# Eight single PSUM banks around the seven-product FFN tiles, six ordinary tiles ahead of them, and adaLN weights in chunks of 1024 columns

## The chip, the cores and the metric

One Trainium2 (trn2) chip, of which the kernel uses 1 core. The metric is the device time in microseconds (us) of one execution, taken as the median of 3 runs. PE is the matmul engine (TensorE), DVE is VectorE, ACT is ScalarE, POOL is GpSimd, and SP is the engine whose queue issues most of the DMAs.

## The reference

The reference is one step of a two-layer recurrent decoder trunk, on a prompt of 512 tokens and on 8 samples of one token, 1024 features wide. Cut to what the change touches:

```python
mod = einsum('bd,de->be', silu(c), w_ada[l]) + b_ada[l]      # 6 chunks of 1024 per layer
sh_m, sc_m, gt_m, sh_f, sc_f, gt_f = split(mod, 6)
out = mixer(x * (1 + sc_m) + sh_m)                           # layer 0 even, layer 1 odd
x = layer_norm(ALPHA * x + (1 + gt_m) * out)
gate, up = split(einsum('bld,df->blf', x * (1 + sc_f) + sh_f, ffn_w_in[l]), 2)
x = layer_norm(ALPHA * x + (1 + gt_f) * einsum('blf,fd->bld', silu(gate) * up, ffn_w_out[l]))
```

`ffn_w_in[l]` is 1024 x 5632 (2816 gate and 2816 up columns, or 22 tiles of 128 of each), and all data are float32.

## The kernel before

Activations lie transposed, features on partitions, as tiles of 128 x 2 x 260: two halves of 256 prompt tokens and 4 samples. Each float32 product is made of three fast matmuls: a weight is split into a rounded part ("hi", a cast on ACT) and a remainder ("lo", a subtraction on DVE), an activation likewise, and PE adds hi*hi, hi*lo and lo*hi in PSUM (`mm3`, lines 284 to 288). The split costs ACT and DVE work for each weight, as well as PE three matmuls.

**Order of the work.** Weights come in the order of one list, `plan`, which is written out by hand. `WS.take` makes the split of the next unit with high priority and loads one entry ahead, into a ring of 3 raw buffers of 1 MB ("raw"); all its loads go through SP's queue (L208, L213). A scheduler at build time lays out one fixed order per engine from the priorities; at run time each engine goes through its order and waits for semaphores. A section under `high_priority(offset=3000)` goes ahead of ordinary work when both are ready.

**PSUM.** There are 8 banks of 2 KB per partition. `psum(2, 4, "g")` holds for the whole kernel: 2 tiles "acc" of two banks each (`acc_tile`) and 4 tiles "mx" of one bank (`mx`). A buffer is taken again once the tile before in it has been read for the last time.

**The adaLN rows** (`mod`) are made in the gaps of the plan. An "ada" entry is 128 rows x 2048 columns of `w_ada`; `ada_part` (L370) multiplies it in four column groups of the array at a time, 512 columns wide. After 8 entries `ada_rows` copies the sum out of PSUM, transposes it in 4 blocks into another mx tile and adds the bias. There are 40 entries: 16 in the even mixer, 16 in the first FFN, 8 in the input projection of the odd mixer.

**The seven-product tiles** are in the second layer's FFN alone. For tiles f = 0 to 3 (`SW0 = 4`) a tile is made the old way: one gate and one up unit of 8 x 6 matmuls, 96 in all. From f = 4 on, `sw_unit` (lines 929 to 967) treats gate and up columns, the two halves of the contraction and the two token halves as a 2 x 2 by 2 x 2 block product with seven multiplications (Strassen-Winograd form). Each is 12 matmuls (`prod`, lines 939 to 941), 84 in all. The activation sums `t1` to `t4` are made once (`t_forms`, 28 DVE operations). The weight sums are made for each tile by the generator `sw_weights`, in four steps: w1, then w2 with four sums in place in the raw buffer, then wu, then wg. The first step is made when the tile before is taken, and one more at each `ws.more()` inside that tile. w1 and w2 take their halves from a ring of 3 buffers ("whi", "wlo"); wu and wg from a ring of 4 ("wxh", "wxl").

In one tile the products run in this order: a (w1 lower), e (wu upper), b (wg lower, on top of a copy of a), a (w1 upper, on top), b (wu lower, on top), d (wg upper, on top of b + p5), c (w2 upper, on top of a copy of b). `o1` holds a and d, `o2` holds c and b, and e is an mx tile. At the end the gate `silu(o1)` is multiplied by the up values `o2`, and the product is split into ah and al for the second FFN matmul. The first half of the FFN (hb = 0) ends with tile 10, the second runs over tiles 11 to 21. In the first half ACT also does one `affine` of x per tile.

Of the kernel before, what the change touches and what calls it, by code (L numbers as in the profile page):

```python
# [35 lines left out]
SW0 = 4  # L36
# [4 lines left out]
def build(tc, I, O):  # L41
    nc = tc.nc
    V, S, G, T, SY = nc.vector, nc.scalar, nc.gpsimd, nc.tensor, nc.sync
    with ExitStack() as ctx:
# [86 lines left out]
        def bc(ap, shape):  # L131
            return ap.to_broadcast(shape)
# [49 lines left out]
        class WS:  # L182
# [77 lines left out]
            def ada(self):  # L260
                while self.i < len(units) and plan[units[self.i][0]][0] == "ada":
                    p_, _, r = self.take()
                    if p_[2] == 0:
                        self.acc = mx()
                    ada_part(self.acc, p_[2], r)
                    if p_[2] == 7:
                        ada_rows(self.acc, p_[6], p_[4] // 128)
# [27 lines left out]
        def p_ada(l, js):  # L295
            return [("ada", I["w_ada"][l], k, 1, D * j, 2 * D, l) for j in js for k in range(8)]
# [35 lines left out]
        plan += mix(p_cols("out", ev_out, (0, 256)), E4[4:6], 1) + E4[6:] + p_cols("out", ev_out, (512, 768))  # L332
# [35 lines left out]
        def ada_part(p, k, r):  # L368
            for c in range(4):
                T.matmul(p[32 * c:32 * c + 32, 0:512], condT[:, k, :], r[:, 0, 512 * c:512 * c + 512],  # L370
                         start=(k == 0), stop=(k == 7), tile_position=(0, 32 * c), skip_group_check=True)

        def ada_rows(p, l, j):
            sb = tmp.tile([128, 512], F32, tag="t2k", name="adarow")
            S.copy(sb, p)
# [3 lines left out]
            tt(mod[l][:, j:j + 16, :].rearrange("p (c b) r -> p b c r", b=4),  # L379
               q.rearrange("p (b c r) -> p b c r", b=4, r=32)[:, :, :, 0:9],  # L380
               bc(vA[:, 48 * l + j:48 * l + j + 16].rearrange("p (c b) -> p b c", b=4).unsqueeze(3), [128, 4, 4, 9]), ALU.add)
# [27 lines left out]
        ctx.enter_context(psum(2, 4, "g"))  # L409
# [472 lines left out]
        def ffn(l, mid=None):  # L882
            with tc.tile_pool(name=f"ff{l}", bufs=1, reuse_waits="tile") as fp:
# [47 lines left out]
                def sw_unit(f):  # L931
                    w1, w2, wu, wg = ws.get("sw", 128 * f)
                    t1, t2, t3, t4, b11, b21, b22 = tf
                    o1, o2, e = acc_tile(), acc_tile(), mx()[:, :HN]
                    a_, d_, c_, b_ = o1[:, 0, :HN], o1[:, 1, :HN], o2[:, 0, :HN], o2[:, 1, :HN]

                    def prod(out, w, off, t, st):
                        for k in range(4):
                            T.matmul(out, w[0][:, off + k], t[0][:, k], start=st and k == 0, stop=False, skip_group_check=True)  # L939
                            T.matmul(out, w[1][:, off + k], t[0][:, k], start=False, stop=False, skip_group_check=True)  # L940
                            T.matmul(out, w[0][:, off + k], t[1][:, k], start=False, stop=k == 3, skip_group_check=True)  # L941

                    soon = lambda: tc.high_priority(offset=HIGH)
                    prod(a_, w1, 0, b11, True)
                    with soon():
                        S.copy(b_, a_)
                    prod(e, wu, 4, t1, True)
                    p5 = t2k("p5")[:, 0]
                    with soon():
                        S.copy(p5, e)  # L950
# [12 lines left out]
                    with soon():  # L963
                        add(b_, b_, p5)
                    m = f % 11
                    fin_ev(0, m, 0, o1[:, :, :HN])
                    fin_ev(1, m, 0, o2[:, :, :HN])

                for hb in range(2):
# [12 lines left out]
                    def fin_ev(up, d, j, acc, hs=BOTH):  # L982
                        m = d + j
                        if up == 0:
# [3 lines left out]
                            if hb == 0 and 3 <= m <= 10:  # L988
                                affine(last["act"], [m - 3])
# [1138 lines left out]
        ffn(1)  # L2128

# [30 lines left out]
```

## Time and profile before

| what | value |
|---|---|
| runs | 1416.21 us median of 3 (1413.34 to 1416.77) |
| the profiled execution | 1415.38 us, of which the span is 1413.3 |
| PE, DVE, ACT, POOL busy | 94%, 62%, 39%, 14% of the span |
| granted TensorE clock, mean | 0.974 |
| DMA | 185 MB, q1 busy 37.4% of 16 engines' span |

A matmul's row shows its duration in the pipeline (0.28 us for 260 columns). Matmuls overlap, so the pace is read from starts, and idle time in a row of PE counts from the end of the duration, not from the time at which the next could have started. The number in brackets at the end of a timeline row is that idle time and what ended it.

### The profile page before, as it was taken

How to read it: one execution, taken by the hardware profiler on the slowest of the kernel's cores; microseconds unless marked ns; L12 is line 12 of the kernel's file. 1: busy time of each engine (PE TensorE's matmuls, PEld its weight loads, DVE VectorE, ACT ScalarE, POOL GpSimd, SP SyncE). 2: the span in 40 equal slices, each digit the busy share in tenths (PEclk: the TensorE clock that was granted, in tenths of full speed). 3: DMA queues.
4: the chain of work that ended last, by engine and by line, in shares of the span. 5: the costliest groups of instructions: out<-in, count | busy, mean ns of one | idle time of the engine just before them, and what ended most of it. 6: DMA issues, size and time to landing. Idle time of an engine off the chain costs nothing. (4 is left out here: it accounts for less than half of the span.)

```text
span 1413.3 us, 28868 instructions
## 1 busy us (share of the span) xinstructions
PE 1323.4 (94%) x12159; PEld 1237.9 (88%) x12159; DVE 875.0 (62%) x1947; ACT 555.9 (39%) x957; POOL 192.7 (14%) x215
## 2 busy tenths in 40 slices
PE   6898999989999999999998999999978899888996
PEld 4797986989998999999987989889978899888996
DVE  4667664687897233323682785677687634777465
ACT  3545535453333222222353223364445522555331
POOL 2200010350011200000250331114200000000013
PEclk9999999999999999999998999999979999999997
DMA  9653364313346742335449446532213133232311
GB/s 282 187 175 131 133 222 141 107 54 109 130 160 218 227 156 98 136 131 180 152 177 195 139 143 206 137 98 65 85 30 90 54 112 98 82 90 72 123 61 61
DMA packets 169147, 185.48 MB, mean 131 GB/s; under 512 B 18444, under 2 KB 153994, under 8 KB 163642
## 3 DMA queue, kind: packets, MB, share of 16 engines
q1 hardware_dynamic: 163034, 166.43, 37.4%
q0 software_dynamic: 5744, 17.08, 3.8%
q8 instruction: 95, 1.56, 0.4%
q14 instruction: 34, 0.28, 0.1%
q10 hardware_dynamic: 240, 0.13, 0.0%
HBM read 167.11 MB, written 15.36 MB: 129 GB/s over the span
## 5 line engine op out<-in xcount | busy, mean ns | idle before, releaser
L111 DVE TENSOR_TENSOR wlo<-raw,whi 128x1024 fp32r<-128x1024 f32 (+2 forms) x216 | 212.2, 993 | 179.5 <-ACT whi L242 133.6
L242 ACT CAST whi<-raw 128x1024 fp32r<-128x1024 f32 (+2 forms) x162 | 149.9, 933 | 419.6 <-PE acc L286 284.7
L284 PE MATMUL acc<-hhi,whi 128*128 128x260 f32 x1360 | 283.4, 289 | 2.7 <-ACT whi L242 1.3
L286 PE MATMUL acc<-hlo,whi 128*128 128x260 f32 x1360 | 282.6, 288 | 0.9 <-DVE hlo L111 0.9
L288 PE MATMUL acc<-hhi,wlo 128*128 128x260 f32 x1360 | 278.3, 285 | 0.0
L284 PEld LDWEIGHTS acc<-hhi,whi 128*128 128x128 f32 x1360 | 211.6, 190 | 22.9 <-issue 9.6
L286 PEld LDWEIGHTS acc<-hlo,whi 128*128 128x128 f32 x1360 | 212.4, 190 | 5.3 <-issue 2.1
L288 PEld LDWEIGHTS acc<-hhi,wlo 128*128 128x128 f32 x1360 | 211.8, 190 | 2.0 <-issue 1.3
L286 PE MATMUL acc<-al,whi 128*128 128x260 f32 x576 | 116.1, 283 | 3.3 <-DVE al L111 3.3
L284 PE MATMUL acc<-ah,whi 128*128 128x260 f32 x576 | 117.3, 285 | 1.0 <-DVE x L123 0.8
L288 PE MATMUL acc<-ah,wlo 128*128 128x260 f32 x576 | 114.9, 282 | 0.0
L284 PEld LDWEIGHTS acc<-ah,whi 128*128 128x128 f32 x576 | 88.7, 188 | 5.1 <-issue 2.6
L286 PEld LDWEIGHTS acc<-al,whi 128*128 128x128 f32 x576 | 88.7, 188 | 3.7 <-DVE al L111 3.5
L288 PEld LDWEIGHTS acc<-ah,wlo 128*128 128x128 f32 x576 | 88.3, 188 | 0.0
L111 DVE TENSOR_TENSOR smp<-acc,gt 128x8 f32<-128x8 f32 (+1 forms) x72 | 11.6, 161 | 117.6 <-PE acc L288 91.7
L863 PE MATMUL acc<-hhi,whi 128*128 128x260 f32 x208 | 59.9, 289 | 3.3 <-ACT hhi L821 3.3
L111 DVE TENSOR_TENSOR wxl<-raw,wxh 128x512 fp32r<-128x512 f32 (+1 forms) x82 | 62.1, 771 | 1.2 <-ACT wxh L242 1.0
L160 ACT CAST whi<-raw 128x512 fp32r<-128x512 f32 x54 | 31.7, 620 | 78.8 <-issue 50.7
L865 PE MATMUL acc<-hlo,whi 128*128 128x260 f32 x208 | 59.0, 291 | 3.2 <-DVE hlo L814 1.8
L111 DVE TENSOR_TENSOR sg<-acc,sg 128x520 f32<-128x520 f32 (+1 forms) x48 | 30.9, 651 | 45.7 <-PE acc L288 41.1
L864 PE MATMUL acc<-hhi,wlo 128*128 128x260 f32 x208 | 59.0, 286 | 0.0
L939 PE MATMUL acc<-hhi,whi 128*128 128x260 f32 x144 | 43.2, 300 | 10.1 <-DVE acc L111 10.1
(636 smaller groups left out, 2932.2 us busy)
## 6 DMA issues: line engine op xcount, KB each, us to landing
raw<-in_w_ada_dram SPq DMA_DIRECT2D x40, 1024.0 KB, 5.3
raw<-in_ffn_w_in_dram SPq DMA_DIRECT2D x24, 1024.0 KB, 5.0
raw<-in_ffn_w_in_dram SPq DMA_DIRECT2D x40, 512.0 KB, 3.9
raw<-in_ffn_w_out_dram SPq DMA_DIRECT2D x16, 1024.0 KB, 5.2
raw<-in_ev_w_in_dram SPq DMA_DIRECT2D x10, 1024.0 KB, 8.4
raw<-in_od_w_in_dram SPq DMA_DIRECT2D x10, 1024.0 KB, 5.7
raw<-in_w_ada_dram SPq DMA_DIRECT2D x16, 512.0 KB, 7.1
raw<-in_ffn_w_out_dram SPq DMA_DIRECT2D x16, 384.0 KB, 3.0
```

The lines of the kernel that those rows point to most:

```text
L111: V.tensor_tensor(out=out, in0=a, in1=b, op=op)
L160: S.copy(t[0][:, q], src[:, q])
L242: S.copy(hi[:, :nk, :m], rj)
L284: T.matmul(acc[:, hf, :HN], wh[:, k - koff, :], ah(k)[:, hf, :], start=st, stop=False)
L286: T.matmul(acc[:, hf, :HN], wh[:, k - koff, :], al(k)[:, hf, :], start=False, stop=False)
L288: T.matmul(acc[:, hf, :HN], wl[:, k - koff, :], ah(k)[:, hf, :], start=False, stop=sp)
L863: T.matmul(out, wh[:, k, :], ah(k)[:, hf, :], start=n == 0, stop=False)
L864: T.matmul(out, wl[:, k, :], ah(k)[:, hf, :], start=False, stop=False)
L865: T.matmul(out, wh[:, k, :], al(k)[:, hf, :], start=False, stop=n == len(ks) - 1)
L939: T.matmul(out, w[0][:, off + k], t[0][:, k], start=st and k == 0, stop=False, skip_group_check=True)
```

## The change

`SW0` becomes 6, so tiles 4 and 5 go the old way. Around the seven-product tiles of each FFN half the pool of acc and mx tiles is closed and a pool of 8 single banks is opened; after them acc and mx are opened anew. Each of a, e, b, d and c takes a bank of its own. The gate and up values are taken out of PSUM by halves, as soon as their product is done, with high priority; b + p5 goes to SBUF (over p5) and not to PSUM. The adaLN entries become 256 rows x 1024 columns, 4 to a chunk: 12 in the even mixer (chunks 2 to 4 of layer 0), 16 in the first FFN, 12 in the odd mixer's input projection. Their transposes go into the free half of the same bank.

```diff
-SW0 = 4
+SW0 = 6
@@ plan
-            return [("ada", I["w_ada"][l], k, 1, D * j, 2 * D, l) for j in js for k in range(8)]
+            return [("ada", I["w_ada"][l], k0, 2, D * j, D, l) for j in js for k0 in range(0, 8, 2)]
-        E2, E4 = p_ada(0, [2]), p_ada(0, [4])
-        FA, FB, OA = p_ada(1, [0]), p_ada(1, [2]), p_ada(1, [4])
+        FA = p_ada(0, [5]) + p_ada(1, [0])
+        FB = p_ada(1, [1, 2])
+        OA = p_ada(1, [3, 4, 5])
-        plan += mix(p_cols("in", ev_in, EV_COLS), E2 + E4[:4])
+        plan += mix(p_cols("in", ev_in, EV_COLS), p_ada(0, range(2, 4)))
@@ ada_part, ada_rows
-            for c in range(4):
-                T.matmul(p[32 * c:32 * c + 32, 0:512], condT[:, k, :], r[:, 0, 512 * c:512 * c + 512],
+            for k in range(2):
+                for c in range(4):
+                    T.matmul(p[32 * c:32 * c + 32, 0:256], condT[:, k0 + k, :], r[:, k, 256 * c:256 * c + 256],
...
-            q = mx()
-            for b in range(4):
-                transpose(q[:, 128 * b:128 * b + 128], sb[:, 128 * b:128 * b + 128])
+            for b in range(2):
+                transpose(p[:, 256 + 128 * b:384 + 128 * b], sb[:, 128 * b:128 * b + 128])
@@ sw_unit
-                    o1, o2, e = acc_tile(), acc_tile(), mx()[:, :HN]
-                    a_, d_, c_, b_ = o1[:, 0, :HN], o1[:, 1, :HN], o2[:, 0, :HN], o2[:, 1, :HN]
+                    bank = lambda: ps["S"].tile([128, 1, 512], F32, tag="sb", name="sb")[:, :, :HN]
+                    a_, e_, b_ = bank(), bank(), bank()
...
                     prod(b_, wg, 0, t2, False)
+                    d_ = bank()
                     with soon():
                         add(d_, b_, p5)
                     prod(a_, w1, 4, b21, False)
+                    with soon():
+                        fin_ev(0, m, 0, a_, slice(0, 1))
                     ws.more()
                     prod(b_, wu, 0, t3, False)
-                    ws.more()
+                    c_ = bank()
                     with soon():
                         S.copy(c_, b_)
+                        add(p5, b_, p5)
+                    ws.more()
                     prod(d_, wg, 4, b22, False)
+                    with soon():
+                        fin_ev(0, m, 0, d_, slice(1, 2))
+                        mul(sg[m][:, 1:2], p5, sg[m][:, 1:2])
                     ws.more()
                     prod(c_, w2, 4, t4, False)
                     with soon():
-                        add(b_, b_, p5)
-                    m = f % 11
-                    fin_ev(0, m, 0, o1[:, :, :HN])
-                    fin_ev(1, m, 0, o2[:, :, :HN])
+                        mul(sg[m][:, 0:1], c_, sg[m][:, 0:1])
+                        split(ah[:, m], al[:, m], sg.pop(m))
@@ ffn
-                        for f in range(max(SW0, f0), f0 + 11):
-                            sw_unit(f)
+                        pg.close()
+                        with tc.tile_pool(name=f"pS{hb}", bufs=8, space=PSUM, reuse_waits="tile") as ps["S"]:
+                            for f in range(max(SW0, f0), f0 + 11):
+                                sw_unit(f)
+                        pg.enter_context(psum(2, 4, f"g{hb}"))
```

## Rows read from the trace of the kernel before

**Rows 1.** The page's second part: PE, granted clock and DMA in 40 slices.
```profile
PE   6898999989999999999998999999978899888996
...
PEclk9999999999999999999998999999979999999997
DMA  9653364313346742335449446532213133232311
```

**Rows 2.** Windows: the stretch, then busy (count) by engine, granted clock, DMA share, GB/s.
```profile
1035.96:1060.25 24.29, 15.75 (x87) 14.72 (x86) 20.90 (x34) 10.18 (x20) 0.00 (x0) 0.65 0.15 43
1060.25:1132.13 71.88, 64.24 (x506) 61.27 (x505) 49.45 (x83) 37.92 (x76) 0.00 (x0) 1.00 0.25 77
1195.74:1326.71 130.97, 117.43 (x926) 112.83 (x925) 93.15 (x158) 64.53 (x127) 1.15 (x2) 1.00 0.30 91
540.00:600.00 60.00, 60.00 (x501) 58.43 (x500) 18.90 (x20) 16.02 (x20) 0.00 (x0) 1.00 0.36 124
...
1077.61:1089.93 12.32, 10.81 (x84) 10.24 (x85) 9.02 (x15) 6.61 (x13) 0.00 (x0) 1.00 0.29 84
...
1224.81:1236.82 12.01, 10.71 (x84) 10.27 (x84) 8.98 (x15) 6.13 (x12) 0.00 (x0) 1.00 0.30 87
```

**Rows 3.** PE's waits in the second half's seven-product tiles: total us, times, longest.
```profile
PE acc L939 <- ACT acc L946: 7.6, 10, 0.8
PE acc L939 <- DVE acc L111: 5.9, 11, 0.6
```

**Rows 4.** Timeline of PE within one tile of the second half.
```profile
1226.24 0.28 PE L941 MATMUL acc<-hlo,whi 128*128 128x260 f32 x1
...
1233.45 0.28 PE L941 MATMUL mx<-t1l,wxh 128*128 128x260 f32 x1
1234.50 0.38 PE L939 MATMUL acc<-t2h,wxh 128*128 128x260 f32 x1 [0.77 <-ACT acc L946]
1234.72 0.37 PE L940 MATMUL acc<-t2h,wxl 128*128 128x260 f32 x1
...
1236.01 0.28 PE L941 MATMUL acc<-t2l,wxh 128*128 128x260 f32 x1
1236.82 0.39 PE L939 MATMUL acc<-hhi,whi 128*128 128x260 f32 x1 [0.53 <-DVE acc L111]
```

**Rows 5.** Timeline of DVE in the same tile.
```profile
1227.26 0.69 DVE L111 TENSOR_TENSOR wlo<-raw,whi 128x512 fp32r<-128x512 f32 x1 [2.50 <-ACT whi L160]
...
1231.56 0.68 DVE L111 TENSOR_TENSOR raw<-raw 128x512 f32<-128x512 f32 x1
1232.15 1.29 DVE L111 TENSOR_TENSOR wlo<-raw,whi 128x512 fp32r<-128x512 f32 x2
1233.36 0.69 DVE L111 TENSOR_TENSOR sg<-acc,sg 128x520 f32<-128x520 f32 x1
1233.97 1.28 DVE L111 TENSOR_TENSOR wxl<-raw,wxh 128x512 fp32r<-128x512 f32 x2
1235.17 0.69 DVE L111 TENSOR_TENSOR al<-sg,ah 128x520 fp32r<-128x520 f32 x1
```

**Rows 6.** PE's timeline in the first seven-product tile: the rows with idle time.
```profile
1039.04 0.39 PE L940 MATMUL mx<-t1h,wxl 128*128 128x260 f32 x1 [1.36 <-DVE wxl L111]
1043.29 0.58 PE L941 MATMUL mx<-t1l,wxh 128*128 128x260 f32 x1 [3.14 <-DVE t1l L111]
1048.15 0.58 PE L940 MATMUL acc<-t2h,wxl 128*128 128x260 f32 x1 [3.41 <-DVE wxl L111]
```

**Rows 7.** Groups of half and whole gate operations: count, busy us, mean ns, idle before.
```profile
L79 ACT ACTIVATE sg<-acc 128x260 f32<-128x260 f32 x6 | 2.1, 379 | 2.7 <-PE acc L865 2.7
L79 ACT ACTIVATE sg<-acc 128x520 f32<-128x520 f32 x10 | 6.1, 608 | 1.3
L111 DVE TENSOR_TENSOR sg<-acc,sg 128x260 f32<-128x260 f32 x4 | 1.5, 421 | 2.7 <-PE acc L865 2.7
L111 DVE TENSOR_TENSOR sg<-acc,sg 128x520 f32<-128x520 f32 x10 | 6.9, 693 | 0.0
L384 ACT CAST ah<-sg 128x520 fp32r<-128x520 f32 x10 | 6.3, 630 | 0.0
```

**Rows 8.** Timeline of PE: two adaLN entries of 512 columns; eight matmuls of 256.
```profile
84.37 1.92 PE L370 MATMUL mx<-raw,condT 128*32 128x512 f32 x16
86.22 0.50 PE L284 MATMUL acc<-hhi,whi 128*128 128x260 f32 x2
...
40.74 1.07 PE L360 MATMUL mx<-raw,condT 128*32 128x256 f32 x16 [1.75 <-DMA raw<-in_w_ada_dram]
41.74 0.66 PE L148 MATMUL mx<-ident,xin 128*128 128x128 f32 x4
```

**Rows 9.** SP's issues at the start of the odd mixer, and PE's wait for them.
```profile
746.02 0.38 SPq L213 DMA_DIRECT2D raw<-in_od_w_in_dram  x1
746.45 0.57 SPq L1817 DMA_DIRECT2D Ud<-ut  x1
747.12 0.39 SPq L213 DMA_DIRECT2D raw<-in_w_ada_dram  x1
747.69 0.79 SPq L1817 DMA_DIRECT2D Ud<-ut  x1
...
757.65 5.42 SPq L1839 DMA_DIRECT2D u<-Ud  x8
...
771.92 0.59 PE L1858 MATMUL mx<-u,bt 128*64 128x72 f32 x5 [6.55 <-DMA u<-Ud]
```

**Rows 10.** The page's sixth part: DMA issues, size, median us to landing.
```profile
raw<-in_w_ada_dram SPq DMA_DIRECT2D x40, 1024.0 KB, 5.3
```

More of the change, by code (lines that the diff above doesn't have):

```diff
@@ L366, in ada_mm, with ada_part @@
             return p[:, 256:288].rearrange("p (c r) -> p c r", r=16)[:, :, 0:9]
[L368 to L381 removed]
+        def ada_part(p, k0, r):
+            for k in range(2):
+                for c in range(4):
+                    T.matmul(p[32 * c:32 * c + 32, 0:256], condT[:, k0 + k, :], r[:, k, 256 * c:256 * c + 256],
+                             start=(k0 + k == 0), stop=(k0 + k == 7), tile_position=(0, 32 * c), skip_group_check=True)
+        def ada_rows(p, l, j):
+            sb = tmp.tile([128, 256], F32, tag="t2k", name="adasb")
+            S.copy(sb, p[:, 0:256])
+            for b in range(2):
+                transpose(p[:, 256 + 128 * b:384 + 128 * b], sb[:, 128 * b:128 * b + 128])
+            tt(mod[l][:, j:j + 8, :].rearrange("p (c b) r -> p b c r", b=2),
+               p[:, 256:512].rearrange("p (b c r) -> p b c r", b=2, r=32)[:, :, :, 0:9],
+               bc(vA[:, 48 * l + j:48 * l + j + 8].rearrange("p (c b) -> p b c", b=2).unsqueeze(3), [128, 2, 4, 9]), ALU.add)
         def split(hi, lo, src):
@@ L407, in exp_ref @@
             stt(out, p, 1.0, out, ALU.add, ALU.mult)
-        ctx.enter_context(psum(2, 4, "g"))
+        pg = ExitStack()
+        pg.enter_context(psum(2, 4, "g"))
         kap = cst.tile([128, 4], F32, name="kap")
@@ L933, in sw_unit @@
                     t1, t2, t3, t4, b11, b21, b22 = tf
-                    o1, o2, e = acc_tile(), acc_tile(), mx()[:, :HN]
-                    a_, d_, c_, b_ = o1[:, 0, :HN], o1[:, 1, :HN], o2[:, 0, :HN], o2[:, 1, :HN]
+                    bank = lambda: ps["S"].tile([128, 1, 512], F32, tag="sb", name="sb")[:, :, :HN]
+                    a_, e_, b_ = bank(), bank(), bank()
                     def prod(out, w, off, t, st):
                         for k in range(4):
-                            T.matmul(out, w[0][:, off + k], t[0][:, k], start=st and k == 0, stop=False, skip_group_check=True)
-                            T.matmul(out, w[1][:, off + k], t[0][:, k], start=False, stop=False, skip_group_check=True)
-                            T.matmul(out, w[0][:, off + k], t[1][:, k], start=False, stop=k == 3, skip_group_check=True)
+                            T.matmul(out[:, 0], w[0][:, off + k], t[0][:, k], start=st and k == 0, stop=False, skip_group_check=True)
+                            T.matmul(out[:, 0], w[1][:, off + k], t[0][:, k], start=False, stop=False, skip_group_check=True)
+                            T.matmul(out[:, 0], w[0][:, off + k], t[1][:, k], start=False, stop=k == 3, skip_group_check=True)
                     soon = lambda: tc.high_priority(offset=HIGH)
+                    m = f % 11
                     prod(a_, w1, 0, b11, True)
@@ L946, in sw_unit @@
                         S.copy(b_, a_)
-                    prod(e, wu, 4, t1, True)
-                    p5 = t2k("p5")[:, 0]
+                    prod(e_, wu, 4, t1, True)
+                    p5 = t2k("p5")[:, 0:1]
                     with soon():
-                        S.copy(p5, e)
+                        S.copy(p5, e_)
                     prod(b_, wg, 0, t2, False)
+                    d_ = bank()
                     with soon():
@@ L987, in fin_ev @@
                             act(sg[m][:, hs], acc, AF.Silu)
-                            if hb == 0 and 3 <= m <= 10:
+                            if hb == 0 and hs.stop == 2 and 3 <= m <= 10:
                                 affine(last["act"], [m - 3])
@@ L2128, in build @@
         ffn(1)
+        pg.close()
 _INS = ['x_prompt', 'x_sample', 'c_prompt', 'c_sample', 'state_gla', 'state_rglru_conv', 'state_rglru_h',
```

4 lines of the change are left out of this document (2 added, 2 removed).

## The prediction

> **What bounds the kernel now.** I read the page's slices first: PE is at nine tenths or more nearly everywhere and its clock is full, so the time is the PE stream plus the places where PE waits. The digits fall to 7 and 8 in slices 30 to 32 and to 8 in slices 35 to 38 [rows 1]; both are the seven-product tiles of the second FFN. The windows put sizes on that. In a plain stretch PE starts 501 matmuls in 60 us, 0.1198 us each. The seven-product tiles take 24.3 + 71.9 = 96.2 us for the 7 tiles of the first half and 131.0 us for the 11 of the second; a steady tile takes 12.3 us in the first half and 12.0 in the second [rows 2]. At the plain pace its 84 matmuls are 10.06 us, and the 96 of a tile made the old way are 11.50. So the clever tile is at present the slower one, and some 2 us of each are waits. No engine beside PE is full there: DVE is busy 9.0 of 12.0 us, ACT 6.1 [rows 2].
>
> The waits of the second half are two per tile, for an ACT copy and for a DVE addition [rows 3]. The timeline says which [rows 4]. Between 1233.45 and 1234.50 PE waits for the copy of a into b; b lies in o2, and o2 of the tile before is read last by the gate multiplication that DVE ends at 1234.05 [rows 5]. Start to start this is 1.05 us where 0.12 is usual, and the next two starts are 0.1 late each: 1.13 us. Between 1236.01 and 1236.82 the second product on a waits for the addition that writes d, another bank but the same tile o1: 0.69 us, with the late start behind it 0.80. Together 1.93, which is 12.02 less 10.06.
>
> **The part that matters, the banks.** The second wait has no reason left once a and d are different tiles: the addition then has the second product on a, 12 x 0.12 = 1.44 us, to hide behind, and needs 0.44. The product b that follows would overwrite what the addition reads, so it waits in its place if DVE is late, which is the thing to watch. That is 0.80 us per tile. With 5 banks per tile out of 8, the bank for b was last used by c two tiles before, so the first wait too loses its reason.
>
> But a third constraint lies right behind it. The remainder of wg, which that same product b needs, is ready only when DVE has ended the first of the pair begun at 1233.97, about 1234.65, that is 0.15 us after PE was let go [rows 4, 5]. That remainder ends a chain which starts from PE itself: w2 of the next tile takes the buffer of w1, which is free when the second product on a ends (start 1226.24, + 0.28 = 1226.52) [rows 4]; then come a cast, the sums in the raw buffer and the splits of wu and wg on DVE, begun at 1227.26 and almost without a gap [rows 5]. From 1226.52 to 1234.65 are 8.13 us. From the remainder back to the end of the second product on a are 24 matmuls and a drain, 2.9 + 0.28. So with DVE's order as it is, the tile cannot fall below 8.13 + 3.18 = 11.3 us, and the gain is 0.7, not 1.93.
>
> How much shorter the chain gets depends on the order in which the scheduler lays DVE's work. Ahead of the wg pair stand two wlo of the tile after next, 1.2 us at a pitch of 0.6, which nobody needs for another tile [rows 5]. With both behind it, the tile comes to 10.1, the floor of PE; with one, to 10.7. The diff raises the gate multiplications and the split of the result to high priority, and does the b + p5 sum earlier, so the order will be drawn anew. Splitting the silu and the multiplication in halves costs 2 x 0.379 - 0.608 = 0.15 us on ACT and 2 x 0.421 - 0.693 = 0.15 on DVE [rows 7], both inside engines that have a quarter of the tile free [rows 2]. I take 10.7, the middle of 10.1 and 11.3, since the rows give no reason for either end.
>
> Second half: 131.0 - 11 x 10.7 = 13.3 us gained (6.7 at 11.3, 20.3 at 10.06).
>
> First half: tiles 4 and 5 the old way are 2 x 11.50 = 23.0. The first seven-product tile, 24.3 us today, keeps its three waits of 1.36, 3.14 and 3.41 us for t1 and the weight splits [rows 6] and the slowed clock after them (0.65 over its window [rows 2]), since `t_forms` goes in the same number of instructions ahead of it; without the addition's wait 23.5. Four more tiles at 10.9 (today 0.3 longer than in the second half, of which I keep 0.2) are 43.6. Sum 90.1 against 96.2: 6.1 gained (3.3 at 11.6 per tile, 9.5 at 10.06). If the two old tiles let DVE get ahead, the first tile's three waits, 7.9 us, are what could still be gained; if `t_forms` meets more work, I allow as much as its largest wait, 3.4, lost.
>
> **Closing and opening the PSUM pools.** Twice in and twice out, each tile waits for the last reader of its bank. The nearest row is such a reader, the half multiplication of 0.42 us [rows 7]. Between nothing and 4 x 0.42 = 1.7 us; I take 0.5, as the first products of each stage use banks long read.
>
> **The adaLN entries.** Two entries of today take PE 86.22 - 84.37 = 1.85 us, 0.93 each; the eight matmuls of 256 columns at 40.74, the same shape as a new entry, take 1.00 [rows 8]. So 40 entries cost from nothing to 3 us more; part of the 1.00 is the end of the last pass, which two entries in a row share, so I take nothing. The transposes stay 20. The copies become 10 of half the size, off PE's path.
>
> Four entries move from the even to the odd mixer, whose list is then 12 entries for 10 of the projection, with one ahead of all. A load lands in 5.3 us [rows 10], and SP's queue keeps its order. There the kernel waits once for the round trip of u through memory, 6.55 us, with two weight loads issued among its writes [rows 9]. One more load among them costs up to 5.3 us; one load fewer there gains as much. I take 1.0 lost.
>
> **The sum.** 13.3 + 6.1 - 0.5 - 1.0 = 17.9 us off the profiled execution of 1415.4 gives 1397.5. The median of the three runs lies 0.8 above that execution: **1398**.
>
> **The rivals.**
>
> *PE's floor.* The weight chain gets out of the way and both halves run at 10.06 us: 20.3 + 9.5 - 1.5 = 28.3 off, 1388. For it: DVE needs only 9.0 us per tile [rows 2], and two of the operations ahead of the wg pair are early by a tile [rows 5]. Against it: in the first half the wait for wxl is there today, beside a PSUM wait that is small. The Trainium skill, Perfetto Trace Analysis, section on identifying performance opportunities, says that the same gap repeating on the engine that should be full can mean that there is not enough SBUF or PSUM for the next tile. By that reading more banks would end the gaps and the time would be this one. The gaps here do repeat, and one of the two ends with a PSUM tile's last reader, but the ready time of wxl says that the ring of weight buffers is as short. Chance 0.27.
>
> *The same order.* DVE keeps its order and the chain of 8.13 us stands: tiles of 11.3 and 11.6, 6.7 + 3.3 - 1.5 = 8.5 off, 1408. For it: the order comes from the same priorities among the weights. Chance 0.17.
>
> *The wait stays.* The addition holds up PE for another reason than the shared tile, or the product b takes the wait over in full. Then tiles stay at 12.0 and 12.3: 23.0 + 24.3 + 4 x 12.3 = 96.5, nothing gained, 1.5 lost: 1418, within 0.3%. Against it: the row names the addition as what ended the wait, in every tile [rows 3]. Chance 0.09.
>
> *Slower: the raised work gets into the chain.* Silu, multiplications and the split of the result go under high priority, where the weight splits already are. If the cast of ah (0.63) [rows 7] and the subtraction of al (0.69), today behind the wg pair [rows 5], go ahead of the splits of wu and wg, the 8.13 us become 9.4 and the tile 12.6. The point from which it decides is 0.7 us of such work in the chain, what the freed addition gives. At 12.6 and 12.9: 131.0 - 138.6 = 7.6 lost in the second half, 23.0 + 23.5 + 51.6 = 98.1, so 1.9 in the first, and 1.5: 11.0 slower, 1427. For it: DVE already has no gap in the chain. Against it: the weight sums come earlier in the program than that split and win between equals. Chance 0.14.
>
> **How the numbers follow.** The forecast has 0.33, PE's floor 0.27, the same order 0.17, the stayed wait 0.09, the slower case 0.14. The first three are faster by more than 0.3%, 4 us, about what a measurement of this kernel tells from no change: 0.77. Within it lies the stayed wait, 0.09; slower is 0.14. The first three alone would leave out 0.23, so the range takes in the stayed wait too: from 1384 (PE's floor with some of the first tile's waits gone) to 1418. The same order with one load of 5.3 us in the way, less the 1.0 already counted, is 1412 and lies inside.
>
> **What would show it.** Right: the tile's distance in the second half is 10.5 to 10.9, the wait for "DVE acc" in front of the second product on a is gone, what is left stands in front of the product b and names wxl; tiles 4 and 5 take 11.5 each; the first seven-product tile keeps two waits of over 3 us. PE's floor is shown by a distance of 10.1 without a wait, the same order by 11.3 and wlo still ahead of the wg pair, the slower case by the al subtraction ahead of it. Wrong beyond these: a longer wait for u at the start of the odd mixer, or a first tile much shorter than 23 us.

## The result and the profile after

The changed kernel takes **1402.8 us** (median of 4 runs, 1400.0 to 1406.4); the kernel before, run beside it on the same chip, 1414.8 us (4 runs, 1412.4 to 1416.8). The ratio is 0.9917, with a 95% interval of 0.9888 to 0.9946. The profiled execution of the changed kernel took 1406.4 us with a span of 1404.6. The two profiles differ by 8.7 us of span, and the table below accounts for those.

The page of the changed kernel, second part (compare [rows 1]):

```profile
PE   6898999999999999999988989999897999999996
...
PEclk9998999999999999999999999999999999999998
```

The dips at the seven-product tiles have shrunk to one 7 in slice 31; the nines of the second half (slices 35 to 37, the only eights there before) are new. Fresh eights stand at slices 21 and 24, in the odd mixer, and at 29. The windows give the sizes, first those of the changed kernel (columns as in [rows 2]):

```profile
1075.85:1139.08 63.23, 54.62 (x421) 53.48 (x421) 50.86 (x90) 33.32 (x70) 0.00 (x0) 0.92 0.26 80
1202.43:1318.53 116.10, 112.42 (x926) 111.36 (x925) 94.20 (x170) 64.40 (x138) 1.15 (x2) 1.00 0.34 102
...
699.20:938.20 239.00, 219.18 (x2645) 204.09 (x2644) 149.08 (x329) 83.78 (x150) 62.83 (x65) 0.95 0.60 175
...
0.00:209.20 209.20, 187.25 (x2282) 161.27 (x2283) 134.72 (x381) 100.58 (x179) 26.47 (x49) 0.96 0.53 165
209.20:699.20 490.00, 481.33 (x4095) 459.78 (x4095) 277.04 (x655) 163.71 (x254) 51.94 (x56) 1.00 0.44 144
...
938.20:1075.85 137.65, 129.22 (x1003) 124.93 (x1002) 87.62 (x173) 64.13 (x110) 29.29 (x27) 0.98 0.22 70
```

Then those stages of the kernel before that were not shown yet:

```profile
700.00:924.60 224.60, 213.64 (x2514) 197.93 (x2513) 148.18 (x327) 83.68 (x148) 64.57 (x65) 0.95 0.59 167
213.60:700.00 486.40, 475.86 (x3916) 450.66 (x3915) 276.79 (x652) 164.09 (x251) 54.23 (x56) 1.00 0.43 143
0.00:213.60 213.60, 193.18 (x2273) 162.57 (x2274) 134.67 (x381) 101.11 (x179) 26.41 (x49) 0.96 0.59 187
...
924.60:1035.96 111.36, 104.80 (x812) 100.54 (x811) 78.37 (x164) 54.68 (x97) 30.28 (x27) 0.98 0.22 68
```

A stage is cut at the first matmul of a layer normalization or of a product tile. PE's count gives the moved work away: the odd mixer starts 2645 matmuls where it was 2514.

| stage | before, us | after, us | difference |
|---|---|---|---|
| even mixer | 213.6 | 209.2 | -4.4 |
| first FFN | 486.4 | 490.0 | +3.6 |
| odd mixer | 224.6 | 239.0 | **+14.4** |
| second FFN, up to the end of tile 10 | 111.4 + 96.2 | 137.7 + 63.2 | -6.7 |
| second FFN, tiles 11 to 21 | 131.0 | 116.1 | **-14.9** |
| everything else | | | -0.8 |

So the second FFN gave more than the change as a whole shows, and the odd mixer took over half of it back.

**The second half's tiles.** Starts of the products lie 10.1 and 11.1 us apart in turn (10.55 on average, 12.0 before). Where [rows 3] had two waits per tile, the changed kernel has one in every other tile:

```profile
PE sb L941 <- DVE sb L111: 3.7, 5, 0.7
```

PE's timeline of the changed kernel shows what differs between two neighbouring tiles (`hhi,whi` is the second product on a, `t2` with `wxh`/`wxl` is the product b with wg, `hhi,wxh` the next product on b, with wu):

```profile
1215.38 0.28 PE L941 MATMUL sb<-hhi,whi 128*128 128x260 f32 x1
...
1216.34 0.28 PE L941 MATMUL sb<-t2h,wxh 128*128 128x260 f32 x1
...
1218.15 0.28 PE L943 MATMUL sb<-t2l,wxh 128*128 128x260 f32 x1
1219.17 0.39 PE L941 MATMUL sb<-hhi,wxh 128*128 128x260 f32 x1 [0.74 <-DVE sb L111]
...
1226.47 0.28 PE L941 MATMUL sb<-t2h,wxh 128*128 128x260 f32 x1
1226.59 0.29 PE L941 MATMUL sb<-hhi,whi 128*128 128x260 f32 x1
...
1229.37 0.28 PE L941 MATMUL sb<-hhi,wxh 128*128 128x260 f32 x1
```

In the first of these tiles the scheduler has put most of the second product on a ahead of the product b, so b ends last, at 1218.15 + 0.28. Only then can DVE write d = b + p5 (it begins at 1218.68, behind a `wlo`), and the next product would overwrite b: PE waits 0.90 us beyond its pace, and 0.11 more with the late start behind it. In the second tile most of the second product on a stands behind b, as the program has it, and covers the addition. DVE in the same two tiles:

```profile
1218.07 0.69 DVE L111 TENSOR_TENSOR wlo<-raw,whi 128x512 fp32r<-128x512 f32 x1 [0.30 <-ACT whi L160]
1218.68 0.43 DVE L111 TENSOR_TENSOR sb<-sb,p 128x260 f32<-128x260 f32 x1
1219.02 2.86 DVE L111 TENSOR_TENSOR raw<-raw 128x512 f32<-128x512 f32 x4
...
1223.34 1.28 DVE L111 TENSOR_TENSOR wxl<-raw,wxh 128x512 fp32r<-128x512 f32 x2
...
1225.88 1.29 DVE L111 TENSOR_TENSOR wlo<-raw,whi 128x512 fp32r<-128x512 f32 x2 [0.22 <-ACT whi L160]
...
1228.43 0.44 DVE L111 TENSOR_TENSOR sb<-sb,p 128x260 f32<-128x260 f32 x1 [0.65 <-PE sb L943]
```

The wg pair of `wxl` (1223.34) now stands ahead of the two `wlo` (1225.88); in [rows 5] it stood behind them. (In the first of the two tiles only the half that product b needs does.) Its first half ends at about 1224.0, 2.4 us before product b starts, and in the second half PE waits for no weight.

**The first seven-product tile.** PE's rows with idle time in the changed kernel, the first at the start of the new pool:

```profile
1075.85 0.39 PE L941 MATMUL sb<-hhi,whi 128*128 128x260 f32 x1 [1.71 <-DVE sg L111]
...
1081.31 0.39 PE L943 MATMUL sb<-t1l,wxh 128*128 128x260 f32 x1 [1.36 <-DVE t1l L111]
...
1086.17 0.59 PE L942 MATMUL sb<-t2h,wxl 128*128 128x260 f32 x1 [3.99 <-DVE wxl L111]
...
1090.86 0.56 PE L941 MATMUL sb<-hhi,wxh 128*128 128x260 f32 x1 [1.93 <-DVE sb L111]
```

**The odd mixer.** PE's waits there, in the kernel before:

```profile
PE mx L1858 <- DMA u<-Ud: 6.5, 1, 6.5
PE acc L286 <- DVE y5l L111: 1.7, 1, 1.7
...
PE mx L148 <- ACT vt L1106: 0.9, 1, 0.9
```

and in the changed kernel:

```profile
PE mx L1870 <- DMA u<-Usd: 7.9, 1, 7.9
PE mx L1220 <- DVE s L123: 3.2, 1, 3.2
PE mx L148 <- ACT vt L1118: 3.2, 1, 3.2
PE mx L372 <- DMA raw<-in_w_ada_dram: 1.7, 1, 1.7
...
PE mx L148 <- ACT adasb L377: 0.8, 1, 0.8
```

By the windows, 8.9 of the 14.4 us are more idle time of PE and 5.5 more busy time. The wait for u is 1.4 us longer; the rest of the idle time is spread over single waits, two of them for the adaLN entries themselves. Of the busy time, 4.9 us are the entries' own matmuls. The entries' matmuls in the same stage (group by line and shape: count, busy us, mean ns), before and then after:

```profile
L370 PE MATMUL mx<-raw,condT 128*32 128x512 f32 x64 | 8.6, 624 | 0.0
```

```profile
L372 PE MATMUL mx<-raw,condT 128*32 128x256 f32 x192 | 13.5, 404 | 1.7 <-DMA raw<-in_w_ada_dram 1.7
```

### The profile page after: what moved, and what is told of

It is laid out like the page before. It is cut to its first block, busy times and chain, and to the rows that moved or that the text cites. A ratio compares the mean times of both kernels' runs of the same rounds, so it can differ in the third digit from the quotient of the medians.

```text
span 1404.6 us, 29570 instructions
## 1 busy us (share of the span) xinstructions
PE 1321.8 (94%) x12503; PEld 1251.7 (89%) x12503; DVE 865.9 (62%) x1946; ACT 549.4 (39%) x962; POOL 187.8 (13%) x215
## 4 chain that ended last, share of the span: by engine, by line
PE 75%; DVE 10%; DMA 7%; issue 3%; ACT 2%; POOL 1%; SPq 1%; POOLq 0%; ACTq 0%; DVEq 0%
PE acc L286 15%; PE acc L284 15%; PE acc L288 15%; PE sb L941 4%; PE sb L943 3%; PE sb L942 3%; PE acc L865 3%; PE acc L867 3%; PE acc L866 3%; PE mx L372 2%; DVE wlo L111 2%; PE mx L148 2%; DMA raw<-in_w_ada_dram 2%; DVE x L111 1%; DMA raw<-in_ffn_w_out_dram 1%
## 5 line engine op out<-in xcount | busy, mean ns | idle before, releaser
L284 PE MATMUL acc<-hhi,whi 128*128 128x260 f32 x1424 | 294.4, 288 | 3.2 <-ACT hhi L79 0.9
L286 PE MATMUL acc<-hlo,whi 128*128 128x260 f32 x1424 | 293.9, 287 | 0.6 <-DVE hlo L111 0.6
L288 PE MATMUL acc<-hhi,wlo 128*128 128x260 f32 x1424 | 290.9, 286 | 0.0
L284 PEld LDWEIGHTS acc<-hhi,whi 128*128 128x128 f32 x1424 | 220.6, 190 | 15.0 <-issue 5.9
L286 PEld LDWEIGHTS acc<-hlo,whi 128*128 128x128 f32 x1424 | 221.1, 189 | 4.7 <-issue 2.7
L288 PEld LDWEIGHTS acc<-hhi,wlo 128*128 128x128 f32 x1424 | 221.2, 189 | 2.4 <-issue 1.9
L286 PE MATMUL acc<-al,whi 128*128 128x260 f32 x576 | 116.1, 283 | 0.9 <-DVE al L111 0.9
L111 DVE TENSOR_TENSOR smp<-acc,gt 128x8 f32<-128x8 f32 (+1 forms) x72 | 11.6, 161 | 110.9 <-PE acc L288 85.7
L865 PE MATMUL acc<-hhi,whi 128*128 128x260 f32 x208 | 60.7, 293 | 3.0 <-ACT hhi L823 2.2
L867 PE MATMUL acc<-hlo,whi 128*128 128x260 f32 x208 | 59.9, 295 | 2.0 <-DVE hlo L111 1.6
L866 PE MATMUL acc<-hhi,wlo 128*128 128x260 f32 x208 | 60.1, 291 | 0.0
L111 DVE TENSOR_TENSOR wxl<-raw,wxh 128x512 fp32r<-128x512 f32 (+1 forms) x74 | 56.3, 777 | 5.0 <-ACT wxh L160 2.9
L111 DVE TENSOR_TENSOR sg<-acc,sg 128x520 f32<-128x520 f32 (+1 forms) x32 | 19.8, 630 | 52.1 <-PE acc L288 47.6
L160 ACT CAST wxh<-raw 128x512 fp32r<-128x512 f32 x64 | 38.3, 619 | 29.0 <-PE sb L942 20.2
L372 PE MATMUL mx<-raw,condT 128*32 128x256 f32 x640 | 45.2, 391 | 2.8 <-DMA raw<-in_w_ada_dram 2.8
```

Source lines behind the costliest of these rows:

```text
L111: V.tensor_tensor(out=out, in0=a, in1=b, op=op)
L284: T.matmul(acc[:, hf, :HN], wh[:, k - koff, :], ah(k)[:, hf, :], start=st, stop=False)
L286: T.matmul(acc[:, hf, :HN], wh[:, k - koff, :], al(k)[:, hf, :], start=False, stop=False)
L288: T.matmul(acc[:, hf, :HN], wl[:, k - koff, :], ah(k)[:, hf, :], start=False, stop=sp)
L372: T.matmul(p[32 * c:32 * c + 32, 0:256], condT[:, k0 + k, :], r[:, k, 256 * c:256 * c + 256], start=(k0 + k == 0), stop=(k0 + k == 7), til ...
L865: T.matmul(out, wh[:, k, :], ah(k)[:, hf, :], start=n == 0, stop=False)
```

## The experiments

Each was timed in 3 rounds beside the kernel before, and ratios are to that kernel. Its median on the chips of these runs was 1412.5 to 1413.6 us, 1414.8 beside the changed kernel, so medians of runs on different chips compare within about 2 us. The banks and the adaLN entries can be taken apart, so that came first.

**Banks without the new entries.** The changed kernel with the plan, `ada_part` and `ada_rows` of before.

```diff
-            return [("ada", I["w_ada"][l], k0, 2, D * j, D, l) for j in js for k0 in range(0, 8, 2)]
+            return [("ada", I["w_ada"][l], k, 1, D * j, 2 * D, l) for j in js for k in range(8)]
...
```

> The changed kernel with the adaLN entries, their plan, products and transposes as they were before; the eight banks and the six old-way tiles stay. Theory (the new adaLN entries, four more of them in the odd mixer, cost what is missing there, and the banks give what the tiles show): the odd mixer, from the last layer norm of the first FFN to the first layer norm behind it, takes about 225 us as before and not 239, the even mixer its 4 us more, and the kernel comes to about 1391 us, 12 below the changed one. Rival (the odd mixer's order came out worse by itself, as a ripple of the FFN's change, or by chance): the odd mixer stays near 235 us or more and the kernel near 1402.

Measured: 1389.8 us, ratio 0.9826 (0.9791 to 0.9860). The tiles take 63.1 and 116.1 us as in the changed kernel, and the odd mixer is back at 224.8:

```profile
702.10:926.90 224.80, 212.19 (x2514) 196.76 (x2513) 149.34 (x327) 83.47 (x148) 64.97 (x65) 0.97 0.59 168
```

**The new entries alone**, in the kernel before.

```diff
-        E2, E4 = p_ada(0, [2]), p_ada(0, [4])
-        FA, FB, OA = p_ada(1, [0]), p_ada(1, [2]), p_ada(1, [4])
+        FA = p_ada(0, [5]) + p_ada(1, [0])
+        FB = p_ada(1, [1, 2])
+        OA = p_ada(1, [3, 4, 5])
...
```

> The kernel before with the new adaLN entries alone: PSUM, the number of old-way tiles and the evacuation as before. Theory: the odd mixer grows from 225 to about 238 us, the even mixer shrinks by 4, the second FFN is untouched (tiles of 12.0 us), so 1414.8 + 11 = about 1426 us. Rival (a ripple of the FFN's change): within 4 us of the kernel before.

Measured: 1421.3 us, ratio 1.0062 (1.0037 to 1.0088), 8.6 us above the kernel before beside it (1412.7). That is 5 us under the theory. The even mixer is 7.6 us shorter (206.0), the odd mixer 11.1 longer (235.7). Both halves of the split agree: the entries cost some 9 us in the old kernel and 13.0 (1402.8 - 1389.8) in the new one, or 10.9 if each of these two is taken against the kernel before beside it. The intervals do not tell these figures apart.

**Four ordinary tiles instead of six**, with the banks and the old entries.

```diff
-SW0 = 6
+SW0 = 4
```

> Like the first run (old adaLN entries, eight banks), with four tiles the old way as before in place of six. Theory: a tile is 10.6 us with the banks against 11.5 the old way, and the first seven-product tile keeps its waits (about 21 us), so it is 1.8 us faster than with six: about 1389 us. Rival (two more old-way tiles give DVE time to get ahead, so that the first tile is cheaper with six): a first tile of 24 us or more and a kernel 2 to 6 us slower than with six.

Measured: 1389.7 us, ratio 0.9828 (0.9799 to 0.9858); the seven tiles of the first half take 85.0 us, the first 21.7 (84 matmuls from its first). It ties with six (0.9826), so the 1.8 us of the theory do not show.

**Six ordinary tiles alone**, in the kernel before.

```diff
-SW0 = 4
+SW0 = 6
```

> The kernel before with six old-way tiles, nothing else. Theory: two tiles of 12.3 become two of 11.5, the first tile keeps about 24 us: 1.6 us faster, 1413 us, with tiles of 12.0 in the second half. Rival (the old-way tiles let DVE get ahead): the first seven-product tile falls from 24 to 21 us as in the changed kernel, and the kernel comes to about 1410.

Measured: 1412.1 us, ratio 0.9990 (0.9973 to 1.0007): a tie, and the interval has room for the 1.6 us of the theory. The first tile takes 23.4, so the rival's 21 does not come.

**The product order pinned.** Banks, old entries, and a dependency without a wait that keeps the scheduler from laying the second product on a ahead of the last matmul of product b.

```diff
+                            if k == 0 and after is not None:
+                                tc.add_manual_dep(i.ins, after.ins.name, NOSYNC, reason="product order")
...
-                    prod(b_, wg, 0, t2, False)
+                    pb = prod(b_, wg, 0, t2, False)
...
-                    prod(a_, w1, 4, b21, False)
+                    prod(a_, w1, 4, b21, False, pb)
```

> Banks with the old adaLN entries and six old-way tiles (the first run), where the second product on a is made to come after the product b on PE, as it stands in the source. In the changed kernel every second tile has it ahead of b, and then the product on b behind it waits 0.9 us for the addition that writes d. Theory (the reordered products alone cost the 1.0 us of every second tile, and the weight chain has slack): all tiles take 10.1 us, 5 x 1.0 fewer in the second half, so 111 us there in place of 116, and the kernel comes to about 1383. Rival (the weight chain that the prediction worked out binds; the reordering only filled its gap): tiles stay at 10.6 or more on average, now with the wait in front of b for wxl, and the time stays within 2 us of 1390.

Measured: **1380.9 us**, ratio 0.9772 (0.9749 to 0.9794), faster than both kernels. In the second half PE has no wait at all and all tiles lie 10.06 to 10.09 us apart; the first half takes 60.6 us:

```profile
1186.72:1297.63 110.91, 110.91 (x926) 110.91 (x925) 92.01 (x170) 64.81 (x138) 1.15 (x2) 1.00 0.34 105
1062.85:1123.40 60.55, 54.30 (x420) 53.37 (x421) 50.57 (x90) 33.58 (x70) 0.00 (x0) 0.92 0.24 74
```

So the 5.2 us between 116.1 and 110.9 are the reordered products, and nothing else holds up the tile in the second half. The first tile of the first half keeps its waits, 3.4 us for `wxl`, 2.8 for `t1l` and 1.7 at the new pool. DVE in that kernel:

```profile
1228.88 0.68 DVE L111 TENSOR_TENSOR wxl<-raw,wxh 128x512 fp32r<-128x512 f32 x1
...
1229.82 1.28 DVE L111 TENSOR_TENSOR wlo<-raw,whi 128x512 fp32r<-128x512 f32 x2
1231.02 0.69 DVE L111 TENSOR_TENSOR wxl<-raw,wxh 128x512 fp32r<-128x512 f32 x1
...
1232.23 0.43 DVE L111 TENSOR_TENSOR sb<-sb,p 128x260 f32<-128x260 f32 x1
```

The half of wg that product b needs ends at 1229.56, 0.5 us before the first matmul that reads it (1230.06 on PE); only the half for product d stands behind the two `wlo`.

**Banks with the late evacuation**: gate and up values leave PSUM at the end of the tile, at ordinary priority, and b + p5 goes back to PSUM.

```diff
-                    with soon():
-                        fin_ev(0, m, 0, a_, slice(0, 1))
...
-                        add(p5, b_, p5)
...
+                        add(b_, b_, p5)
+                    fin_ev(0, m, 0, a_, slice(0, 1))
+                    fin_ev(0, m, 0, d_, slice(1, 2))
```

> Banks with the old adaLN entries and six old-way tiles, but the values taken out at the end of the tile and with ordinary priority, and b + p5 in PSUM, as before: the banks alone. Theory (the banks take both waits away, the early evacuation adds little): a tile of 10.1 to 10.8 us, 1390 to 1393 us. Rival (the raised and halved evacuation is what redraws DVE's order; with the order of before the weight chain holds 11.3 us): tiles of 11.3 and a kernel of about 1400.

Measured: 1389.3 us, ratio 0.9829 (0.9805 to 0.9852); tiles of 10.1 and 10.9 in turn, and in the second half this one wait:

```profile
PE sb L940 <- DVE sb L111: 2.6, 5, 0.5
```

**The early evacuation with the old PSUM tiles** (and six ordinary tiles, old entries). Against the changed kernel, the tiles are bound as before:

```diff
+                    o1, o2, e_ = acc_tile(), acc_tile(), mx().unsqueeze(1)[:, :, :HN]
+                    a_, d_, c_, b_ = o1[:, 0:1, :HN], o1[:, 1:2, :HN], o2[:, 0:1, :HN], o2[:, 1:2, :HN]
```

> The old PSUM layout (a with d, c with b, e in an mx tile), old adaLN entries, six old-way tiles, but the early, halved and raised evacuation of the change: the other half of it. Theory: the wait of the second product on a for the addition stays, 0.8 us per tile, and the next tile's o2 comes free a little earlier: tiles of 11.2 to 12.0 us in the second half, 1403 to 1412 us. Rival (the evacuation is what matters): tiles under 11 us and about 1392.

Measured: 1412.3 us, ratio 0.9993 (0.9972 to 1.0015). The tile takes 12.2 us, a little more than the theory allowed, with two waits again:

```profile
PE acc L941 <- DVE wxl L111: 7.1, 9, 0.8
PE acc L940 <- DVE acc L111: 6.6, 11, 0.6
```

DVE in one of these tiles, and PE at the product b that waits:

```profile
1237.15 1.29 DVE L111 TENSOR_TENSOR wlo<-raw,whi 128x512 fp32r<-128x512 f32 x2
1238.36 0.69 DVE L111 TENSOR_TENSOR wxl<-raw,wxh 128x512 fp32r<-128x512 f32 x1
...
1239.10 0.39 PE L941 MATMUL acc<-t2h,wxl 128*128 128x260 f32 x1 [0.78 <-DVE wxl L111]
```

The banks are the whole gain, and no gain of the evacuation shows, by itself or with them. The first of these waits is the weight chain of the prediction: both `wlo` still stand ahead of the wg half that product b needs. So the raised evacuation by itself did not bring the `wlo` behind it. With the banks that happened, with the late evacuation too: there a `wxl` of 1218.23 stands ahead of the two `wlo` of 1219.17, and no weight is waited for in the second half. Why the scheduler lays it so is not shown.

The second of these waits comes although a and d lie in different banks; it goes as soon as they are different tiles. The Trainium skill, PSUM — Partial Sum Buffer, section on bank collisions, has the rule that PSUM needs guarding by bank and quadrant of partitions, so an access to another bank needs none. By that rule the wait was the bookkeeping by whole tiles and not the chip's need; the pair of runs agrees, 6.6 us in the second half with the shared tile and none in front of that product with single banks.

**The new shape at the old counts.** The remaining question is what of the adaLN change costs: the four moved entries or the shape. Here the shape is new, and 16, 16 and 8 entries lie where they did before.

```diff
-        FA = p_ada(0, [5]) + p_ada(1, [0])
-        FB = p_ada(1, [1, 2])
-        OA = p_ada(1, [3, 4, 5])
+        FA = p_ada(1, [0, 1])
+        FB = p_ada(1, [2, 3])
+        OA = p_ada(1, [4, 5])
...
```

> The changed kernel with its new adaLN entries (256 rows by 1024 columns), but placed as before: 16 in the even mixer, 16 in the first FFN, 8 in the odd mixer. Theory (the four entries more in the odd mixer cost there 3.7 us of PE and some 7 of waits in SP's order, the shape nothing): about 1391 to 1393 us, with the odd mixer at 225 to 228 us. Rival (the shape costs: twice the weight loads, twice the copies, each bank held through its transposes): the odd mixer stays near 235 and the kernel at 1400 or more.

Measured: 1398.7 us, ratio 0.9900 (0.9871 to 0.9929). My theory missed: by the medians the shape costs 8.9 us of the 13.0 (1398.7 against 1389.8). The entries' matmuls in the odd mixer are 0.6 us longer than before; that stage is 233.0, with a lower granted clock:

```profile
705.00:938.00 233.00, 219.51 (x2578) 205.47 (x2577) 149.92 (x328) 83.98 (x149) 63.79 (x65) 0.94 0.55 162
```

```profile
L372 PE MATMUL mx<-raw,condT 128*32 128x256 f32 x128 | 9.2, 386 | 0.0
```

The stage is 8.2 us longer than without the new entries (224.8), and 7.3 of these are busy time of PE (219.51 against 212.19). Most of that goes with the granted clock: the stretches at 0.50, the lower of its two levels (1.2 and 2.4 GHz), take longer here. Two of them in this kernel, and then one of the kernel without the new entries:

```profile
851.60:858.40 6.80, 6.80 (x34) 6.80 (x33) 0.90 (x9) 0.90 (x4) 0.00 (x0) 0.50 0.47 130
913.00:926.70 13.70, 13.23 (x60) 12.27 (x59) 9.50 (x25) 3.59 (x5) 5.14 (x8) 0.50 0.59 184
```

```profile
904.00:910.80 6.80, 6.80 (x31) 6.57 (x31) 6.21 (x18) 1.89 (x4) 1.99 (x3) 0.50 0.25 77
```

If half of PE's busy time in such stretches is counted as lost (an estimate from the granted clock), the odd mixer loses 13.0 us here and 5.8 without the new entries, and the work that is left is the same, 206.5 us in both. PE had been idle for 1.9 us, up to 851.17, before the clock fell at 851.6.

**The new shape in the odd mixer only, and everywhere but there.** Two kernels with both shapes in one plan; the diffs show lines of the plan, against the kernel of the last run.

```diff
-        FA = p_ada(1, [0, 1])
-        FB = p_ada(1, [2, 3])
+        FA, FB = p_old(1, [0]), p_old(1, [2])
         OA = p_ada(1, [4, 5])
...
```

> Banks as in the changed kernel; the adaLN entries of the even mixer and of the first FFN are 128 rows x 2048 columns as before, only the 8 of the odd mixer are 256 x 1024. All old took 1389.8 us with an odd mixer of 224.8; all new at the old counts 1398.7 with 233.0, and an even mixer 4 us longer. Theory A, the shape costs where it lies: odd mixer 232 to 233, first normalization of the even mixer at 213.5, total 1397 to 1399. Rival B, the odd mixer's loss comes from the schedule being drawn anew by entries that lie elsewhere, with the shape itself at its 1.4 us of matmul time: odd mixer 225 to 227, total 1390 to 1392.

```diff
-        OA = p_ada(1, [4, 5])
+        OA = p_old(1, [4])
...
```

> The mirror image: the 16 entries of the even mixer and the 16 of the first FFN are 256 rows x 1024 columns, the 8 of the odd mixer are 128 x 2048. Theory A, the shape costs where it lies: odd mixer 225, first normalization at 217.5, total 1390.5 to 1394 (the even mixer's 4 us less what comes back). Rival B, the schedule: odd mixer 229 or more although its own entries are the old ones, total 1395 or more.

Measured: 1399.6 us, ratio 0.9908 (0.9883 to 0.9934), with the new shape in the odd mixer alone; 1390.0 us, ratio 0.9852 (0.9801 to 0.9903), with the old shape there and the new one in the 32 other entries. By the medians, the 8 entries of the odd mixer carry the whole cost. The profiles are less sharp: the odd mixer takes 231.7 us in the first and 229.5 in the second, whose profiled execution was the longest of its four (1400.8; the others 1384.4 to 1392.0). So in the second kernel the total is theory A's and the odd mixer rival B's, and its even mixer (214.1) is not the 4 us longer that was expected. In the kernels with old entries in this stage and the banks, the odd mixer was 222.0 to 229.5.

Counted as above, the odd mixers with 8 entries, of all runs, hold the same work of PE, 205.7 to 206.9 us, in either shape. What differs is the time lost at the lower clock, 3.9 to 11.1 us with the old shape there and 6.6 to 13.0 with the new one, and PE's idle time, 9.6 to 13.1 against 13.5 to 15.1. The 11.1 are those of the second kernel here, whose four executions show how far the clock goes with the time: 1384.4, 1388.0, 1392.0 and 1400.8 us at a mean granted clock of 0.981, 0.982, 0.975 and 0.969. The first kernel's lie at 1396.8 to 1401.1 with 0.978 to 0.972, so the mean clock alone does not explain the difference.

**The transposes in a bank of their own**, with the new shape at the old counts.

```diff
+            q = mx()[:, 0:256]
             for b in range(2):
-                transpose(p[:, 256 + 128 * b:384 + 128 * b], sb[:, 128 * b:128 * b + 128])
+                transpose(q[:, 128 * b:128 * b + 128], sb[:, 128 * b:128 * b + 128])
```

> The all-new shape at the old counts (1398.7 us, odd mixer 233.0, first normalization at 217.5), with the two transposes of a chunk going into a single-bank tile of their own, as in the kernel before, and not into the free half of the accumulator's bank. Theory C, the longer hold of the bank costs (its copy, transposes and addition keep one of four single banks from the mixer's products): odd mixer 225 to 228, total 1390 to 1394. Rival D, the entries' shape costs and not where they are transposed: odd mixer 231 to 235, total 1396 to 1401.

Measured: 1395.3 us, ratio 0.9879 (0.9819 to 0.9938), with executions from 1385.8 to 1403.9 and an odd mixer of 228.7. That lies between the two theories and its interval takes in both: inconclusive.

**The pinned order with four ordinary tiles** (`SW0 = 4`).

> The kernel with the pinned product order (1380.9 us, entries of before) with four ordinary tiles ahead instead of six. In it every seven-product tile takes 10.08 us where an ordinary one takes 11.5, so two more of them should give 2 x 1.4 = 2.8 us: 1378. Rival: the first seven-product tile gets longer by as much, as its weight sums and activation sums have two tiles less of lead (with unpinned order six and four tied at 1389.8 and 1389.7): 1380 to 1382.

Measured: 1380.2 us, ratio 0.9780 (0.9751 to 0.9810), a tie with six (0.9772). The rival's reason does not show: the first tile takes 18.9 us, against 19.9 with six, and the seven together

```profile
1035.80:1115.53 79.73, 72.95 (x588) 72.35 (x589) 67.84 (x122) 46.84 (x98) 0.00 (x0) 0.96 0.27 82
```

against 60.6 + 2 x 11.5 = 83.6 with six. The 3.9 us that this stage gains are less than what the rest of the kernel varies by.

## Why the prediction was right, and where it was not

**The total**: 1398 forecast, 1402.8 measured, inside 1384 to 1418 and on the expected side. That it lies so near is luck, two errors of opposite sign: against the forecast, the tiles gave 4 us more (22.9 by the run without the new entries, 1412.7 - 1389.8; 18.9 in the sum), the adaLN change took 10 to 12 more (10.9 or 13.0, not 1.0). With 10.9 the sum closes: 22.9 - 10.9 = 12.0 = 1414.8 - 1402.8.

**The second wait goes, since a and d become different tiles**: right, shown by the two runs that change the banks alone and the evacuation alone. The forecast, with the Trainium skill, Perfetto Trace Analysis, section on identifying performance opportunities, read the repeating gaps as a possible want of PSUM; here single banks end both gaps of the steady tiles, but the banks are 8 before and after. So PSUM as such was not short: the first gap was a lack of free tiles of two banks, and the second was two banks tied into one tile.

**The tile at 10.7 in the second half**: 10.55 measured, 14.9 us gained against 13.3. The size is right and the step behind it is wrong. The forecast took the chain of weight sums as the next limit, between 10.1 and 11.3. That limit is real in the old layout, where product b waits 0.8 us for wxl once the evacuation is early; with the banks its own rule, that with both `wlo` behind the wg pair the tile comes to PE's floor, is what happened: the chain binds in no tile of the second half. The forecast looked to the raised evacuation and the earlier b + p5 to redraw DVE's order; the `wlo` moved with the banks. What keeps half of the tiles at 11.1 is the risk named in the same part and priced at nothing, that product b waits in place of the second product on a. The failed sentence is "the addition then has the second product on a, 12 x 0.12 = 1.44 us, to hide behind": it took the order of the products for fixed, while the scheduler was free to interleave two products that no longer share a tile. The pinned order shows the price, 5.2 us here and 2.5 in the first half. Two readings were slightly off and change nothing: 12.02 less 10.06 is 1.96, not 1.93, and the eights of the second half end with slice 37.

**The first half**: 90.1 forecast with two ordinary tiles; 89.5 measured (the 96.2 of before less the table's 6.7: 23.0 for the two ordinary tiles, 1.9 at the new pool, 63.2 for the tiles, and 1.4 of which no part is named). The parts come by another road. The first tile takes 21.0 (84 matmuls from its first), not 23.5: of the waits of [rows 6] the first is gone, the others are 1.36 and 3.99, and an addition adds 1.93. "Tiles 4 and 5 the old way" were priced as such; four or six make no difference that these runs tell, with or without the banks.

**Pools, 0.5 within nothing to 1.7**: one place of the four costs anything. The first product of the first half starts 1.87 us late by its pace (1075.85, idle time 1.71, ended by a gate multiplication on DVE; the same 1.71 stands there in the runs with single banks and old entries); the other three show no gap. The choice was low, and the bound of 1.7 short by 0.2.

**The adaLN entries**, "I take nothing", and one load, "I take 1.0 lost": this is the term that failed, 1.0 against 11 to 13 (8.6 in the old kernel), and the bounds given, 3 and 5.3, do not hold it either. The move of four entries is small beside that: 4.0 us by medians (1402.8 - 1398.7), which the intervals do not tell from nothing. In the odd mixer itself 12 entries of the new shape cost PE about 3 us more work than 8 and 2 to 6 more of idle time (17.3 and 19.8 us in the two kernels with 12), and in the table the even mixer gives back 4.4. The new shape was priced by the matmuls of [rows 8], and that price is right (8.6 us became 9.2 for 8 entries); but it is not where the time went. The 3.6 us of the first FFN are no sign of it: with the new shape there it took 487.5 us at the old counts, with the old one 488.6. Two runs place 9 us, by medians, on the 8 entries of the odd mixer. The profiles show of what kind the loss is: PE's work in the stage is the same, and the time goes into idle time and into stretches at the lower clock. How the shape brings these about stays open: the waits are single and differ from kernel to kernel, the wait for u is even shorter in two of them (3.4 and 4.7 us, against 6.4), old entries too have executions that lose 11 us at the lower clock, and the transposes in their own bank settled nothing. The step that failed is the assumption that an entry of equal PE time is an equal entry for the stage around it.

**Slower, 0.14**: raised work in the chain did not come; the slower part was one that no rival named.

## What to carry to other kernels

Where a timeline shows PE waiting for a write to one half of a two-bank tile, single-bank tiles remove the wait; but they also remove the dependency that kept two products in order, so look at the order that the scheduler then lays, and pin the product that covers an evacuation behind the one that it covers. A bundle of edits can hide a loss inside a gain: cut stages of both traces at the same instructions and add up their differences, before the total is believed. A change of the shape of filler work at equal engine time is not free by that alone; time it alone.

## What the runs showed that was not expected

With single banks and pinned products PE runs the 924 matmuls of 11 tiles in 110.9 us, 0.1200 us each, without one wait (the window's 926 counts two that reach over its ends), while DVE is busy 83% (92.0) and ACT 58% of that time. And the odd mixer took from 222.0 to 229.5 us in the profiles of the kernels that have single banks and the old entries there, with the same work to do, at granted clocks between 0.95 and 0.97: the time lost at the lower clock alone differs by 5 us between them. In this stage a profile of one execution can't settle a question of a few us, and medians of several runs had to.
